# Router weights, gate tiles and gate products rearranged around the end of a mixer and the ranking of a mixture of experts

## Chip, cores and metric

One core of a Trainium2 chip runs the whole kernel as one program. The metric is the device time of one execution in microseconds (us).

## The reference

Two decoder layers over 256 tokens of 1024 channels, all in float32. A layer is a token mixer (differential attention and latent attention, merged by sigmoid gates), a layer norm, and a channel mixer with a gated embedding input. The channel mixer is a dense SwiGLU in layer 0 and a top-2-of-8 mixture of experts in layer 1:

```python
x = layernorm(ALPHA * x + mixer(x))            # ln_mix
h = swiglu(x) or moe(x)                        # layer 0 / layer 1
e = sigmoid(x @ w_ple_gate) * (p @ w_ple_proj) # gated embedding
x = layernorm(ALPHA * x + h + e)               # ln_ffn
```

The mixture takes logits = x @ w_router, the two largest of each token, and softmax gates; each expert is a SwiGLU of width 3584.

## The kernel before

**Products.** Float32 accuracy comes from splitting each operand into a high part (float32r, a cast on ScalarE) and a low part (the remainder, a subtraction on VectorE), and adding three products (`mm3`, L116): one of 128x512 columns is 12 instructions for four blocks of 128 channels. A weight tile is 128x2048 (1 MB): `fetch` (L88) issues its load on the SP queue into one of four raw buffers, `parts` (L97) makes its high part (three buffers) and low part (two buffers), in halves. `stream` (L109) does both. A raw buffer is free again when its low part has been made, a low buffer when the products that read it are over.

**Order.** Outside `manual_schedule` a planner places each instruction on its engine by estimated costs and due times, so work can be drawn ahead of or into other work. Inside `manual_schedule` the instructions keep the order written, but planned ones can be placed between them. Engines run their own instructions in order.

**End of the mixer** (L619 to L645, both layers). The output projection adds w_out tiles into four PSUM banks `yo`. In a manual block: the second half of these products, `ple_product` (L764, 24 products of the embedding, four PSUM banks `prps`), then on VectorE for the two token blocks (tb) the residuals (L340), the start of the norm (L357), the root (L371, eight small steps) and the scaling (L374), which writes x.

**Layer 0 after it** (L1343 to L1352). `transpose_x` (L302) turns x block by block on TensorE and splits it. `ple_out` (L773) copies the embedding sums out of PSUM, which frees the banks that the gate products need. `ple_gate` (L799) streams the four tiles of w_ple_gate, with 24 products each for the two token blocks, and `gate_add` (L782) applies sigmoid and product and adds to x. Then the dense SwiGLU (L806).

**Layer 1 after it** (`before_moe`, L887, all in a manual block). In this order: the router weights are loaded on POOL's queue and split; x is turned and split; the router's 24 products (L904); high parts of the gate tiles on ScalarE, around `ple_out`; `choose` (L933: logits out of PSUM, turned, the two largest); `counts` (L961: five small products); `rank` (L977: experts sorted by load, written as integers `meta`); the low parts of all four gate tiles; `begin` (L1055), which issues the first six expert loads; the 96 gate products; `places` and `select` (which token goes where); the split of x for the gathers; `gate_add`.

**Experts.** An expert's address is read by SP from `meta`, so no expert load can be issued before `rank`. The six raw buffers (four and two extra) give six loads ahead. `run` (L1105) first gathers the tokens of the first pair, then makes high parts four steps and low parts three steps ahead of the products (`cast_hi` L1089, `cast_lo` L1097), and each step asks for one more load (`more`, L1063). There are eight jobs of 42 tiles, small (8 products a tile) and large (12 products a tile); the first is small. In the last job's end the residual sums are combined and the result is normalised and stored.

Memory of closed pools is given to new ones; an instruction that writes to such a place waits for the readers of the old tile.

Of the kernel before, what the change touches and what calls it, by code (L numbers as in the profile page):

```python
# [10 lines left out]
F32 = mybir.dt.float32  # L11
F32R = mybir.dt.float32r
# [8 lines left out]
D = 1024  # L21
# [56 lines left out]
class Net:  # L78
# [18 lines left out]
    def parts(self, raw, a, b):  # L97
        nc = self.nc
        hi = self.wp.tile([128, 2048], F32R, name="whi", tag="whi", bufs=HI_BUFS)
        lo = self.wp.tile([128, 2048], F32R, name="wlo", tag="wlo", bufs=LO_BUFS)  # L100
        step = max(1, self.width // b) * b
        for c0 in range(0, a * b, step):
            s = slice(c0, min(c0 + step, a * b))
            self.latest = nc.scalar.copy(hi[:, s], raw[:, s])  # L104
            with self.after(self.hold.pop() if self.hold else None):
                nc.vector.tensor_tensor(lo[:, s], raw[:, s], hi[:, s], op=OP.subtract)  # L106
        return [[t[:, k * b:(k + 1) * b] for k in range(a)] for t in (hi, lo)]
# [35 lines left out]
    def start(self):  # L143
# [12 lines left out]
        vec = self.vec = cp.tile([12, 128], F32, name="vec")  # L156
        for r0, nr, nm in ((0, 6, "mla_q_norm_g"), (6, 4, "mla_kv_norm_g"), (10, 2, "diff_subln_g")):
            nc.sync.dma_start(vec[r0:r0 + nr], i[nm].rearrange("l (a p) -> (l a) p", p=128))
# [243 lines left out]
    def mixer(self, l):  # L402
# [182 lines left out]
        self.ple_load(l)  # L585
        mh = mp.tile([128, KC, T], F32R, name="mh", tag="dq")
# [24 lines left out]
        def wout(k0, g):  # L611
            return self.stream(self.rows(i["w_out"][l], k0, 4, g * 512, 512), 4, 512)
# [12 lines left out]
        w = [wout(4, g) for g in range(2)]  # L625
# [3 lines left out]
        with self.tc.manual_schedule():  # L629
# [3 lines left out]
            self.ple_product()  # L633
# [9 lines left out]
            self.ln_root(1)  # L643
            for c in range(2):
                self.ln_scale(1, b, u, c)  # L645

# [117 lines left out]
    def ple_product(self):  # L764
        w, p = self.ple
        self.prs = {}
        for tb in range(2):
            for g in range(2):
                ps = self.prs[tb, g] = self.mmp.tile([128, 512], F32, name="prps", tag="mm")
                gs = slice(g * 512, (g + 1) * 512)  # L770
                self.xs(ps, [w[0][:, k, gs] for k in range(2)], [w[1][:, k, gs] for k in range(2)], 0, 2, tb, 2, p)

    def ple_out(self):  # L773
        pr = self.mp.tile([128, 2, D], F32, name="pr")
        for (tb, g), ps in self.prs.items():
            self.nc.scalar.copy(pr[:, tb, g * 512:(g + 1) * 512], ps)
        return pr
# [21 lines left out]
    def ple_gate(self, l, pr):  # L799
        for g in range(2):  # L800
            pss = self.gate_ps()
            for n in (2 * g, 2 * g + 1):
                self.gate_mm(pss, self.stream(*self.gate_tile(l, n)), n)
            self.gate_add(pr, pss, g)
# [69 lines left out]
    def route_tables(self):  # L874
# [10 lines left out]
        self.fold = rp.tile([128, 64], F32, name="fold")  # L885

    def before_moe(self, l, xp):  # L887
        nc, mp, rp, j = self.nc, self.mp, self.rp, l // 2
        self.hold, self.first = [], []
        rw = mp.tile([128, KC, NE], F32, name="rw")  # L890
        nc.gpsimd.dma_start(rw, self.rows(self.i["router_w"][j], 0, KC, 0, NE))
        self.route_tables()
        raws = [self.fetch(*self.gate_tile(l, n)) for n in range(4)]
        self.xp, self.turn = xp, 0
        rwh, rwl = (mp.tile([128, KC, NE], F32R, name=nm) for nm in ("rwh", "rwl"))
        self.split(rwh, rwl, rw)
        nc.vector.tensor_tensor(self.fold, self.ident[:, 0:64], self.ident[:, 64:128], op=OP.add)
# [5 lines left out]
        for k in range(KC):  # L903
            self.mm3(rps[:NE, :T], rwh[:, k], rwl[:, k], self.xh[:, k, :], self.xl[:, k, :], k == 0, k == KC - 1)  # L904
        his, los = ([self.side(nm, F32R, n, own, extra) for n in range(4)]
                    for nm, own, extra in (("whi", HI_BUFS, XHI_BUFS), ("wlo", LO_BUFS, XLO_BUFS)))
        for n in range(2):
            nc.scalar.copy(his[n], raws[n])
        pr = self.ple_out()
        for n in range(2, 4):  # L910
            nc.scalar.copy(his[n], raws[n])
        m, gg, eq = self.choose(rps)
        nc.scalar.activation(gg[:, :, 1:2], gg[:, :, 1:2], AF.Exp)
        cps = self.counts()
        self.rank(cps)
        for n in range(4):
            nc.vector.tensor_tensor(los[n], raws[n], his[n], op=OP.subtract)
        self.begin(j)
        gws = [[[t[n][:, k * 512:(k + 1) * 512] for k in range(4)] for t in (his, los)] for n in range(4)]
        pss = [self.gate_ps() for _ in range(2)]  # L920
        for n in range(4):
            self.gate_mm(pss[n // 2], gws[n], n)
        self.places(cps, m, gg, eq)
        self.sel = rp.tile([128, 2, NP, 256], F32R, name="sel", tag="sel")
        self.select(0)
        self.xth = rp.tile([128, 2, D], F32R, name="xth")
# [3 lines left out]
        for g in range(2):  # L930
            self.gate_add(pr, pss[g], g)
# [123 lines left out]
    def begin(self, j, jobs=None, ahead=RAW_BUFS + XRAW_BUFS):  # L1055
# [3 lines left out]
        self.raws, self.expert = [], {}  # L1059
# [45 lines left out]
    def run(self, done=None, pairs=True):  # L1105
# [6 lines left out]
        self.his, self.los = [], []  # L1112
# [53 lines left out]
        for s in range(ah):  # L1166
            self.cast_hi(s)
            if s < al:
                self.cast_lo(s)
# [157 lines left out]
def body(tc, ins, consts, out, tap=None):  # L1327
# [5 lines left out]
    with pool("const") as cp, pool("small") as sp, pool("weights") as wp, \  # L1333
            tc.tile_pool(name="mm", bufs=MM_BUFS, space=PSUM) as mmp, tc.tile_pool(name="at", bufs=8 - MM_BUFS, space=PSUM) as ap:
        n.cp, n.sp, n.wp, n.mmp, n.ap = cp, sp, wp, mmp, ap
        with pool("bias") as n.bp, pool("xt") as n.tp:
            for l in range(DEPTH):
# [4 lines left out]
                if l % 2 == 0:  # L1342
                    with pool("ffn") as n.mp:  # L1343
                        n.new_xt()
                        for tb in range(2):
                            n.transpose_x(tb)
                        pr = n.ple_out()
                        n.tap(f"x{2 * l}", n.x)
                        n.ple_gate(l, pr)
# [42 lines left out]
```

## Time and profile before

| | us |
|---|---|
| median of 3 runs | 1723.58 (1722.13 to 1727.06) |
| the profiled execution's own time | 1723.58 |
| its span, first to last instruction | 1721.9 |
| TensorE busy | 1639.3 (95%) |
| VectorE busy | 1383.3 (80%) |
| ScalarE busy | 1137.9 (66%) |
| DMA, mean rate over the span | 279 GB/s |

In the profile PE is TensorE's products, PEld its weight loads, DVE VectorE, ACT ScalarE, POOL GpSimd, SP the engine that issues loads. A row names a line of the kernel, an operation, and out<-in by the program's names; what stands in brackets is how long the engine had been idle and what released it. PEclk is the granted share of TensorE's full clock. All times are from the start of the span.

### The profile page before, as it was taken

The page shows a single profiled execution, that of the slowest core. Times are in us where ns is not written, and L with a number is a line of the kernel's source. Part 1 is how long each engine was busy: PE and PEld are TensorE (multiplying, and loading weights), DVE is VectorE, ACT ScalarE, POOL GpSimd, SP SyncE. Part 2 cuts the span into 40 slices and gives each one's busy share as a digit, 9 for nine tenths or more (in the row PEclk, how much of TensorE's full clock was granted, in tenths as well). Part 3 has the DMA queues.
Part 4 walks back from the last instruction along what each step waited for, and adds up shares of the span by engine and source line. Part 5 has one row for each costly group of instructions (what it writes and reads, how often), then busy time and mean ns, then how long its engine had stood idle before and what let it go on. Part 6 is the DMA issues. An engine that isn't in the chain of part 4 may idle for free.

```text
span 1721.9 us, 22472 instructions
## 1 busy us (share of the span) xinstructions
PE 1639.3 (95%) x8152; PEld 1343.8 (78%) x8152; DVE 1383.3 (80%) x1687; ACT 1137.9 (66%) x1366; POOL 43.0 (2%) x39
## 2 busy tenths in 40 slices
PE   8899998999989999978999999999999999999995
PEld 8787787888878887856778887788888877788874
DVE  6987776544567678677999889998888898998997
ACT  5556744434446667347888778877777788777884
POOL 0321000000000000000000000000000000000000
PEclk9999999999989999989999999999999999999998
DMA  7434464555546444635999999999999999999993
GB/s 253 156 123 138 150 214 154 195 185 189 176 131 206 131 151 138 235 147 224 409 403 405 348 380 402 403 409 351 353 367 354 377 399 392 409 406 360 405 404 148
DMA packets 171584, 481.25 MB, mean 279 GB/s; under 512 B 8876, under 2 KB 33592, under 8 KB 171464
## 3 DMA queue, kind: packets, MB, share of 16 engines
q1 hardware_dynamic: 170120, 474.98, 74.3%
q0 software_dynamic: 1344, 4.75, 0.9%
q8 instruction: 66, 1.08, 0.3%
q14 instruction: 54, 0.44, 0.1%
HBM read 478.65 MB, written 1.05 MB: 279 GB/s over the span
## 4 chain that ended last, share of the span: by engine, by line
PE 34%; DMA 9%; DVE 6%; ACT 3%; issue 1%; DVEq 0%; ACTq 0%; SPq 0%
DMA raw<-in_expert_w_dram 9%; PE mps L118 6%; PE mps L120 6%; PE mps L119 5%; DVE wlo L1102 5%; PE macc L118 3%; PE macc L120 3%; PE macc L119 3%; ACT whi L1094 2%; PE mps L1040 2%; PE mps L1041 2%; PE ftp L1240 1%; PE macc L1040 1%; PE macc L1041 1%; PE htp L1244 1%
## 5 line engine op out<-in xcount | busy, mean ns | idle before, releaser
L1102 DVE TENSOR_TENSOR wlo<-raw,whi 128x2048 fp32r<-128x2048 f32 (+1 forms) x338 | 756.4, 2272 | 48.7 <-ACT whi L1094 29.6
L1094 ACT CAST whi<-raw 128x2048 fp32r<-128x2048 f32 (+1 forms) x338 | 637.9, 1907 | 146.6 <-DMA raw<-in_expert_w_dram 58.5
L106 DVE TENSOR_TENSOR wlo<-raw,whi 128x1024 fp32r<-128x1024 f32 (+2 forms) x222 | 259.5, 1190 | 158.0 <-issue 79.3
L104 ACT CAST whi<-raw 128x1024 fp32r<-128x1024 f32 (+2 forms) x222 | 218.6, 1015 | 183.1 <-PE hps L120 51.8
L1040 PE MATMUL mps<-wlo,g 128*128 128x512 f32 x448 | 181.3, 405 | 9.4 <-DVE wlo L1102 7.6
L118 PE MATMUL mps<-wlo,g 128*128 128x512 f32 x448 | 178.2, 398 | 0.4 <-DVE wlo L1102 0.4
L120 PE MATMUL mps<-whi,g 128*128 128x512 f32 x448 | 176.6, 394 | 0.0
L1041 PE MATMUL mps<-whi,g 128*128 128x512 f32 x448 | 176.5, 394 | 0.0
L119 PE MATMUL mps<-whi,g 128*128 128x512 f32 x448 | 175.7, 392 | 0.0
L1040 PEld LDWEIGHTS mps<-wlo,g 128*128 128x128 f32 x448 | 84.6, 189 | 39.2 <-DVE wlo L1102 21.8
L1040 PE MATMUL macc<-wlo,hi 128*128 128x512 f32 x224 | 92.9, 415 | 13.6 <-DVE hi L127 10.9
L120 PEld LDWEIGHTS mps<-whi,g 128*128 128x128 f32 x448 | 84.1, 188 | 20.0
L118 PEld LDWEIGHTS mps<-wlo,g 128*128 128x128 f32 x448 | 84.2, 188 | 19.1 <-DVE wlo L1102 1.1
L119 PEld LDWEIGHTS mps<-whi,g 128*128 128x128 f32 x448 | 84.2, 188 | 18.8
L1041 PEld LDWEIGHTS mps<-whi,g 128*128 128x128 f32 x448 | 84.8, 189 | 17.3
L400 PE MATMUL dqp<-x,whi 128*128 128x512 f32 x256 | 95.6, 414 | 2.2 <-DVE vm L484 2.2
L1041 PE MATMUL macc<-whi,hi 128*128 128x512 f32 x224 | 89.7, 401 | 0.0
L118 PE MATMUL macc<-wlo,hi 128*128 128x512 f32 x224 | 88.6, 395 | 0.0
L120 PE MATMUL macc<-whi,lo 128*128 128x512 f32 x224 | 88.1, 393 | 0.0
L119 PE MATMUL macc<-whi,hi 128*128 128x512 f32 x224 | 87.8, 392 | 0.0
L118 PE MATMUL hps<-wlo,x 128*128 128x512 f32 (+1 forms) x192 | 71.8, 374 | 0.0
L120 PE MATMUL hps<-whi,x 128*128 128x512 f32 (+1 forms) x192 | 71.4, 372 | 0.0
(371 smaller groups left out, 2945.3 us busy)
## 6 DMA issues: line engine op xcount, KB each, us to landing
raw<-in_expert_w_dram SPq DMA_DIRECT2D x336, 1024.0 KB, 8.7
raw<-in_w_in_dram SPq DMA_DIRECT2D x40, 1024.0 KB, 5.1
raw<-in_dense_w_dram SPq DMA_DIRECT2D x33, 1024.0 KB, 5.1
raw<-in_w_branch_diff_dram SPq DMA_DIRECT2D x8, 1024.0 KB, 5.0
raw<-in_w_out_dram SPq DMA_DIRECT2D x8, 1024.0 KB, 5.0
raw<-in_w_ple_gate_dram SPq DMA_DIRECT2D x8, 1024.0 KB, 5.2
raw<-in_w_branch_mla_dram SPq DMA_DIRECT2D x4, 1024.0 KB, 5.3
raw<-in_w_in_dram SPq DMA_DIRECT2D x4, 768.0 KB, 4.8
```

Of the source, the lines that this page charges most:

```text
L104: self.latest = nc.scalar.copy(hi[:, s], raw[:, s])
L106: nc.vector.tensor_tensor(lo[:, s], raw[:, s], hi[:, s], op=OP.subtract)
L118: mm(ps, sh, ml, start=first, stop=False)
L119: mm(ps, sh, mh, start=False, stop=False)
L120: mm(ps, sl, mh, start=False, stop=last)
L400: mm(*one, start=k == 0 and m == 0, stop=end and m == 1)
L1040: mm(ps, st, ml, start=first, stop=False)
L1041: mm(ps, st, mh, start=False, stop=last)
L1094: self.nc.scalar.copy(hi[:, p], raw[:, p])
L1102: self.nc.vector.tensor_tensor(lo[:, p], raw[:, p], self.his[s][:, p], op=OP.subtract)
L1240: nc.tensor.matmul(ps[:, a, q, :], hs[a][n][:, q * 128:(q + 1) * 128], self.fold, start=True, stop=True)
L1244: nc.tensor.transpose(ps[:, q, :], hs[n][:, q * 128:(q + 1) * 128], self.ident)
```

## The change

In layer 0, gate tile 0 is split before the norm and gate tile 1 behind it, at written places; the second of the last two w_out tiles has a low buffer of its own (in memory that the mixer no longer uses); the embedding products are done one token block at a time, with the transposes of x's first block between them; and the gate products of column half 0 run block by block from a manual block. In layer 1, the router weights are loaded in the mixer into a tile of the constants' pool; two gate tiles' high parts and one low part come before the transposes of x; the gate products of tile 0 stand between the router and the ranking, those of the other tiles behind it, with the low parts of tiles 2 and 3 between the steps of the ranking's second half; and the first two expert tiles are split before the experts' loop.

```diff
--- before.py
+++ after.py
@@ -94,10 +94,10 @@
...
-    def parts(self, raw, a, b):
+    def parts(self, raw, a, b, lo=None):
         nc = self.nc
         hi = self.wp.tile([128, 2048], F32R, name="whi", tag="whi", bufs=HI_BUFS)
-        lo = self.wp.tile([128, 2048], F32R, name="wlo", tag="wlo", bufs=LO_BUFS)
+        lo = self.wp.tile([128, 2048], F32R, name="wlo", tag="wlo", bufs=LO_BUFS) if lo is None else lo
         step = max(1, self.width // b) * b
...
@@ -154,6 +154,7 @@
...
         vec = self.vec = cp.tile([12, 128], F32, name="vec")
+        self.rw = cp.tile([128, KC, NE], F32, name="rw")
         for r0, nr, nm in ((0, 6, "mla_q_norm_g"), (6, 4, "mla_kv_norm_g"), (10, 2, "diff_subln_g")):
...
@@ -583,6 +584,8 @@
...
         self.ple_load(l)
+        if not first:
+            nc.gpsimd.dma_start(self.rw, self.rows(i["router_w"][l // 2], 0, KC, 0, NE))
         mh = mp.tile([128, KC, T], F32R, name="mh", tag="dq")
...
@@ -622,7 +625,11 @@
...
                 merged(1)
-        w = [wout(4, g) for g in range(2)]
+        w = [wout(4, 0)]
+        raw = self.fetch(self.rows(i["w_out"][l], 4, 4, 512, 512), 4, 512)
+        w.append(self.parts(raw, 4, 512, mp.tile([128, 2048], F32R, name="wl", tag="kt")))
+        if first:
+            self.gate0 = self.stream(*self.gate_tile(l, 0))
         gbu = mp.tile([128, 2, 2, D], F32, name="gbu", tag="gt")
...
@@ -630,7 +637,10 @@
...
                     self.xs(acc[tb][c], *w[c], 4, 4, tb, KC, (mh, ml))
-            self.ple_product()
+            if first:
+                raw = self.fetch(*self.gate_tile(l, 1))
+            self.prs = {}
+            self.ple_product(0)
             for c in range(2):
...
@@ -641,8 +651,14 @@
...
             self.ln_root(1)
+            if first:
+                self.new_xt()
+                self.transpose_x(0)
+            self.ple_product(1)
             for c in range(2):
                 self.ln_scale(1, b, u, c)
+            if first:
+                self.gate1 = self.parts(raw, 4, 512)
...
@@ -761,20 +777,16 @@
...
-    def ple_product(self):
+    def ple_product(self, tb):
         w, p = self.ple
-        self.prs = {}
-        for tb in range(2):
-            for g in range(2):
-                ps = self.prs[tb, g] = self.mmp.tile([128, 512], F32, name="prps", tag="mm")
-                gs = slice(g * 512, (g + 1) * 512)
-                self.xs(ps, [w[0][:, k, gs] for k in range(2)], [w[1][:, k, gs] for k in range(2)], 0, 2, tb, 2, p)
-
-    def ple_out(self):
-        pr = self.mp.tile([128, 2, D], F32, name="pr")
-        for (tb, g), ps in self.prs.items():
-            self.nc.scalar.copy(pr[:, tb, g * 512:(g + 1) * 512], ps)
-        return pr
+        for g in range(2):
+            ps = self.prs[tb, g] = self.mmp.tile([128, 512], F32, name="prps", tag="mm")
+            gs = slice(g * 512, (g + 1) * 512)
+            self.xs(ps, [w[0][:, k, gs] for k in range(2)], [w[1][:, k, gs] for k in range(2)], 0, 2, tb, 2, p)
+
+    def ple_out(self, pr, tb):
+        for g in range(2):
+            self.nc.scalar.copy(pr[:, tb, g * 512:(g + 1) * 512], self.prs[tb, g])
...
@@ -796,12 +808,23 @@
...
-    def ple_gate(self, l, pr):
-        for g in range(2):
+    def ple_gate(self, l):
+        pr = self.mp.tile([128, 2, D], F32, name="pr")
+        with self.tc.manual_schedule():
+            self.ple_out(pr, 0)
             pss = self.gate_ps()
-            for n in (2 * g, 2 * g + 1):
-                self.gate_mm(pss, self.stream(*self.gate_tile(l, n)), n)
-            self.gate_add(pr, pss, g)
+            self.gate_mm(pss, self.gate0, 0, (0,))
+            self.transpose_x(1)
+            self.gate_mm(pss, self.gate1, 1, (0,))
+            self.ple_out(pr, 1)
+            self.gate_mm(pss, self.gate0, 0, (1,))
+            self.gate_mm(pss, self.gate1, 1, (1,))
+        self.tap(f"x{2 * l}", self.x)
+        self.gate_add(pr, pss, 0)
+        pss = self.gate_ps()
+        for n in (2, 3):
+            self.gate_mm(pss, self.stream(*self.gate_tile(l, n)), n)
+        self.gate_add(pr, pss, 1)
...
@@ -883,18 +906,29 @@
...
         self.fold = rp.tile([128, 64], F32, name="fold")
+        nc.gpsimd.tensor_tensor(self.fold, self.ident[:, 0:64], self.ident[:, 64:128], op=OP.add)
...
         self.hold, self.first = [], []
-        rw = mp.tile([128, KC, NE], F32, name="rw")
-        nc.gpsimd.dma_start(rw, self.rows(self.i["router_w"][j], 0, KC, 0, NE))
         self.route_tables()
...
         self.xp, self.turn = xp, 0
+        his, los = ([self.side(nm, F32R, n, own, extra) for n in range(4)]
+                    for nm, own, extra in (("whi", HI_BUFS, XHI_BUFS), ("wlo", LO_BUFS, XLO_BUFS)))
+        gws = [[[t[n][:, k * 512:(k + 1) * 512] for k in range(4)] for t in (his, los)] for n in range(4)]
+
+        def high(n):
+            nc.scalar.copy(his[n], raws[n])
+
+        def low(n):
+            nc.vector.tensor_tensor(los[n], raws[n], his[n], op=OP.subtract)
+
         rwh, rwl = (mp.tile([128, KC, NE], F32R, name=nm) for nm in ("rwh", "rwl"))
-        self.split(rwh, rwl, rw)
-        nc.vector.tensor_tensor(self.fold, self.ident[:, 0:64], self.ident[:, 64:128], op=OP.add)
+        self.split(rwh, rwl, self.rw)
+        high(0)
+        low(0)
+        high(1)
         self.new_xt()
...
@@ -902,33 +936,38 @@
...
             self.mm3(rps[:NE, :T], rwh[:, k], rwl[:, k], self.xh[:, k, :], self.xl[:, k, :], k == 0, k == KC - 1)
-        his, los = ([self.side(nm, F32R, n, own, extra) for n in range(4)]
-                    for nm, own, extra in (("whi", HI_BUFS, XHI_BUFS), ("wlo", LO_BUFS, XLO_BUFS)))
-        for n in range(2):
-            nc.scalar.copy(his[n], raws[n])
-        pr = self.ple_out()
-        for n in range(2, 4):
-            nc.scalar.copy(his[n], raws[n])
+        low(1)
+        pr = mp.tile([128, 2, D], F32, name="pr")
+        self.ple_out(pr, 0)
+        pss = [self.gate_ps()]
+        self.gate_mm(pss[0], gws[0], 0, (0,))
         m, gg, eq = self.choose(rps)
+        self.gate_mm(pss[0], gws[0], 0, (1,))
+        self.ple_out(pr, 1)
         nc.scalar.activation(gg[:, :, 1:2], gg[:, :, 1:2], AF.Exp)
...
         self.rank(cps)
-        for n in range(4):
-            nc.vector.tensor_tensor(los[n], raws[n], his[n], op=OP.subtract)
+        high(2)
+        high(3)
         self.begin(j)
-        gws = [[[t[n][:, k * 512:(k + 1) * 512] for k in range(4)] for t in (his, los)] for n in range(4)]
-        pss = [self.gate_ps() for _ in range(2)]
-        for n in range(4):
-            self.gate_mm(pss[n // 2], gws[n], n)
+        self.gate_mm(pss[0], gws[1], 1)
+        low(2)
+        pss.append(self.gate_ps())
+        self.gate_mm(pss[1], gws[2], 2)
         self.places(cps, m, gg, eq)
...
         self.select(0)
+        low(3)
         self.xth = rp.tile([128, 2, D], F32R, name="xth")
...
             self.split(self.xth[:, tb], self.xtl[:, tb], self.x[:, tb])
-        for g in range(2):
-            self.gate_add(pr, pss[g], g)
+        self.gate_mm(pss[1], gws[3], 3)
+        self.gate_add(pr, pss[0], 0)
+        for s in range(2):
+            self.cast_hi(s)
+            self.cast_lo(s)
+        self.gate_add(pr, pss[1], 1)
...
@@ -1056,7 +1095,7 @@
...
         self.blocks, self.steps = self.plan(self.jobs)
-        self.raws, self.expert = [], {}
+        self.raws, self.expert, self.his, self.los = [], {}, [], []
         for _ in range(ahead):
...
@@ -1109,7 +1148,6 @@
...
             last[kind, bi, mat] = s
-        self.his, self.los = [], []
         gs, ups, hid, accs, turn = {}, {}, {}, {}, {}
@@ -1163,7 +1201,7 @@
...
         ah, al = HI_BUFS + XHI_BUFS - 1, LO_BUFS + XLO_BUFS - 1
-        for s in range(ah):
+        for s in range(len(self.his), ah):
             self.cast_hi(s)
...
@@ -1341,12 +1379,7 @@
...
                     with pool("ffn") as n.mp:
-                        n.new_xt()
-                        for tb in range(2):
-                            n.transpose_x(tb)
-                        pr = n.ple_out()
-                        n.tap(f"x{2 * l}", n.x)
-                        n.ple_gate(l, pr)
+                        n.ple_gate(l)
                         n.dense(l // 2)
...
                         n.tap(f"x{2 * l + 1}", n.x)
```

## Rows read from the trace of the kernel before

**Rows 1.** The page, busy time of each engine over the whole span
```profile
PE 1639.3 (95%) x8152; PEld 1343.8 (78%) x8152; DVE 1383.3 (80%) x1687; ACT 1137.9 (66%) x1366; POOL 43.0 (2%) x39
```
**Rows 2.** Stretches, layer 0: length, busy us (xcount) by engine, PEclk, DMA share, GB/s
```profile
272.20:280.00 7.80, 3.36 (x19) 2.39 (x17) 6.23 (x15) 3.33 (x7) 1.05 (x2) 0.76 0.82 230
...
280.00:284.00 4.00, 4.00 (x11) 3.21 (x12) 0.83 (x2) 1.86 (x4) 0.00 (x0) 0.61 0.02 6
```
**Rows 3.** Timeline of TensorE, layer 0: start us, us, instruction, [idle before, releaser]
```profile
277.68 1.97 PE L307 MATMUL xps<-ident,x 128*128 128x128 f32 x8 [2.96 <-DVE x L377]
```
**Rows 4.** Timeline of VectorE, layer 0's norm
```profile
261.61 0.69 DVE L344 SCALAR_TENSOR_TENSOR x<-x,yo 128x512 f32<-128x512 f32 x1 [2.02 <-PE yo L120]
...
263.93 1.22 DVE L106 TENSOR_TENSOR wlo<-raw,whi 128x1024 fp32r<-128x1024 f32 x1
```
**Rows 5.** Timeline of VectorE, layer 1's norm
```profile
726.14 0.69 DVE L344 SCALAR_TENSOR_TENSOR x<-x,yo 128x512 f32<-128x512 f32 x1 [0.81 <-PE yo L120]
...
728.86 0.69 DVE L344 SCALAR_TENSOR_TENSOR x<-x,yo 128x512 f32<-128x512 f32 x1 [2.02 <-PE yo L120]
...
736.75 0.75 DVE L377 SCALAR_TENSOR_TENSOR x<-gbu,ly 128x512 f32<-128x512 f32 x1
...
739.13 1.41 DVE L377 SCALAR_TENSOR_TENSOR x<-gbu,ly 128x512 f32<-128x512 f32 x2
```
**Rows 6.** Timeline of TensorE, layer 1, from the mixer to the experts
```profile
739.54 1.91 PE L307 MATMUL xps<-ident,x 128*128 128x128 f32 x16
...
747.44 0.38 PE L118 MATMUL rps<-x,rwh 128*8 128x256 f32 x1 [5.99 <-DVE x L127]
...
752.40 0.29 PE L939 MATMUL rtp<-ident,lt 8*128 8x8 f32 x2 [0.51 <-DVE lt L936]
...
754.37 0.17 PE L964 MATMUL rkp<-memb,ut 128*128 128x8 bf16 x1 [1.68 <-DVE gg L958]
...
758.89 0.76 PE L118 MATMUL plps<-wlo,x 128*128 128x512 f32 x1 [4.24 <-DVE wlo L917]
...
792.18 0.79 PE L1040 MATMUL mps<-wlo,g 128*128 128x512 f32 x1 [4.81 <-DVE wlo L1102]
```
**Rows 7.** Timeline of POOL and ScalarE, layer 1
```profile
739.82 0.90 POOL L891 DMA_DIRECT2D rw<-in_router_w_dram  x1 [20.28 <-PE prps L120]
...
744.74 0.24 ACT L126 CAST rwh<-rw 128x64 fp32r<-128x64 f32 x1 [7.95 <-DMA rw<-in_router_w_dram]
...
744.89 2.04 ACT L126 CAST x<-xps 128x512 fp32r<-128x512 f32 x4
...
746.80 3.73 ACT L908 CAST whi<-raw 128x2048 fp32r<-128x2048 f32 x2
```
**Rows 8.** Busy time in stretches, layer 1 (columns as in rows 2)
```profile
739.50:741.50 2.00, 1.95 (x17) 1.67 (x15) 1.04 (x2) 0.00 (x0) 1.60 (x5) 1.00 0.03 2
...
774.00:778.00 4.00, 4.00 (x19) 3.21 (x18) 0.69 (x1) 0.00 (x0) 0.00 (x0) 1.00 0.18 70
...
800.00:820.00 20.00, 19.41 (x86) 13.89 (x84) 20.00 (x10) 16.88 (x13) 0.00 (x0) 1.00 1.02 409
```
**Rows 9.** Chain that ended last: start us, us, what
```profile
884.70 0.50 PE macc L1040
```
**Rows 10.** Timeline of ScalarE, layer 0
```profile
267.09 2.01 ACT L104 CAST whi<-raw 128x1024 fp32r<-128x1024 f32 x2 [0.72 <-ACT whi L104]
...
292.66 0.60 ACT L787 ACTIVATE plsg<-plps 128x512 f32<-128x512 f32 x1 [2.12 <-PE plps L120]
```
**Rows 11.** Timeline of VectorE, layer 1, before the experts
```profile
745.50 2.48 DVE L127 TENSOR_TENSOR x<-xps,x 128x512 fp32r<-128x512 f32 x4
...
756.37 0.17 DVE L996 CAST meta<-info 128x16 int32<-128x16 f32 x1
...
756.45 8.89 DVE L917 TENSOR_TENSOR wlo<-raw,whi 128x2048 fp32r<-128x2048 f32 x4
...
769.02 2.35 DVE L127 TENSOR_TENSOR xtl<-x,xth 128x1024 fp32r<-128x1024 f32 x2
```

## The prediction, made before the change was run

> **What bounds the kernel now.** I read the page first, then the two stretches that the change touches, engine by engine. TensorE is busy nearly throughout [rows 1], so a gain can only come from the few places where it stands still or runs slowly, and from the stage at the end that it doesn't bound. There are three.
>
> The first is the end of layer 0's mixer. Between 272.2 and 280.0 TensorE works 3.36 of 7.80 us, its clock falls, and the first 4 us of gate products run at 0.61 of full clock [rows 2]. It waits for the normalised x [rows 3]. VectorE is late because four half tiles of gate weights (the low parts of tiles 0 and 1, 1.22 each, the first of the four in the rows [rows 4]) were planned into the chain of the norm. That makes 4.9 us. The same norm in layer 1 has none of them [rows 5].
>
> The second is in front of the router in layer 1. TensorE has nothing for 5.99 us, since the split of x sits on ScalarE behind the split of the router weights, and these were requested at 739.82 and were there at 744.74 [rows 6, 7]. After the ranking it waits 4.24 us for a gate tile's low part.
>
> The third is the start of the experts. All six raw buffers have been filled by about 775 (70 GB/s from 774 to 778), then the queue stands still until the first expert tile's low part is made at 792.15, which frees the first of them; from there loads run at 409 GB/s with the DMA engines full [rows 6, 8]. A tile of 1.0486 MB takes 2.56 us at that rate, against 8 products of the small job, 8 x 0.227 = 1.8 us (12 products of 512 columns take 728.86 - 726.14 = 2.72 us [rows 5]). So the first job's 42 tiles are paced by the loads. Only from 884.7 is the chain TensorE's without a break [rows 9]; a large job's tile is 12 products, 2.72 us, more than its load. Whatever moves the stream of loads earlier moves the rest with it.
>
> **The change, layer 0.** I carry the undisturbed norm of layer 1 over by the residual of the first token block's second half: 728.86 there, 261.61 here, 467.25 us apart [rows 4, 5]. Nothing in front of that residual moves: tile 1 of the second w_out pair gets a low buffer of its own, and gate tile 0 is split in the buffers so freed, before the norm. VectorE then scales the first block's second half until 270.2 and ends the second root at 271.9. TensorE ends the mixer at 261.6 + 2 x 2.72 = 267.0, does the first block's embedding products (12, until 269.7), four transposes (0.12 each at full clock [rows 6]) until 270.2, the other four until 270.8, and the second block's products until 273.5. ScalarE takes the two high parts of x (0.5 each) until 271.4, gate tile 1's high part (2.0 [rows 10]) until 273.4, and the first copy of the embedding sums (0.5), which frees a PSUM bank at 273.9. VectorE, behind the root, makes two low parts (0.62 each) until 273.1, scales the second block (1.41) until 274.5, and makes tile 1's low part (2.4) until 276.9. So gate products start at 274.0: 12 until 276.7, eight transposes until 277.7, 12 with tile 1 until 280.4, 24 more until 285.9. Before, the sigmoid on those 48 products' end starts at 292.66 [rows 10], so they ended at 292.6. That is 6.7 us; TensorE's pauses shrink to some 0.5 us each. Next in line is gate tile 2's low part, whose buffer comes free at 283.1, 2.4 us of split against 2.7 us of products: covered. I take 6.5. The dense stage and layer 1 keep TensorE busy with a load share well under one, so it carries on.
>
> A rule to weigh here: the change puts transposes between products, and the 16 transposes of layer 1, right behind products, ran at 1.00 of full clock, 1.91 us in all [rows 6, 8]; behind a pause of 2.96 us, eight took 1.97 [rows 3]. The Trainium skill (TensorE: Matmul & The Clock Gate, Part 4: PE-mode transpose) says that transposes don't count as work for the clock. By that the 16 would cost 2 us more here and the products behind them start slowly; the trace speaks against it for a run as short as this.
>
> **Layer 1, up to the ranking** (on the old clock). The router weights' load goes onto POOL's queue behind the embedding load and ahead of the two norm vectors; POOL is idle there for 100 us, so it costs nothing and takes away 739.82 to 744.74. But ScalarE's split of them still can't start before the embedding products end, near 739.5: their tile lies where the old one did, and that one's load waited for those products [rows 7]. From 739.5 ScalarE: 0.24, then two gate high parts ahead of the split of x (1.87 each) until 743.5, then x's four high parts (0.51 each) until 745.5. VectorE: tile 0's low part (2.22 [rows 11]) until 743.9, x's low parts (0.62 each), the third at 745.9. The router starts there instead of 747.44, 1.5 us earlier, and ends 4.45 later (747.44 to 751.89 [rows 6]) at 750.4.
>
> Now the products in between: 12 until 753.1, the ranking's two transposes, 12 more until 755.9 (VectorE's choice, 754.37 - 752.40 = 2.0, hides beside them), then the counts, and 2.2 us of ranking (754.37 to the integers at 756.37 + 0.17 = 756.54 [rows 6, 11]) until 758.2. It was 756.5, so the first expert load is asked for **1.7 us later**. All waiting behind: TensorE has no pause of note, so the clock stays up, where before 24 gate products of tile 0 ran behind a sparse stretch.
>
> **From the ranking to the experts.** TensorE: tile 1 until 761.4, tile 2 until 766.8, tile 3 until 772.3. VectorE: tile 2's low part until 760.4, places and selection (from 756.45 + 8.89 = 765.34 to 769.02 = 3.7 [rows 11]) until 764.1, tile 3's low part until 766.3, x's low parts 2.35 until 768.7, the first gate addition (four steps of 0.69) until 771.5, **expert tile 0's low part until 773.8, tile 1's until 776.1**, the second addition until 778.9, tile 2's until 781.2, then one each 2.3. ScalarE has the high parts earlier in each case. Four of the first loads are issued at 759, the fifth at 760.4 and the sixth at 766.3, when the gate tiles' raw buffers come free, so all six are there at about 776.
>
> Before, load seven went out at 792.15, and 36 loads at 2.56 ended at 884.3. After, loads seven and eight go out at 773.8 and 776.1, load nine at 781.2, and from there 34 at 2.56 end at 868.3. **16.0 us earlier.** The fold matrix moved to POOL, the lists moved to begin, and splitting the calls cost nothing: POOL is idle, and the rest issues nothing new.
>
> Sum: 6.5 + 16.0 = 22.5. The profiled execution took 1723.58 us (span 1721.9), which is the median of the three runs: 1723.6 - 22.5 = **1701**.
>
> **Bounds.** Layer 0: at most 7.6 (20.4 us from 272.2 to 292.6, less 1.9 of transposes and 10.9 of products); at least 3, if ScalarE and clock cost as in the first rival. Loads: at most 17.9 (load seven alone: 792.15 - 773.8 = 18.3, less little), at least 10, if each of VectorE's steps behind the ranking waits once more (two extra low parts, 4.5) and the second addition's 2.8 us leave the queue emptier. Below nothing I exclude for the loads: their start has 16 us in hand.
>
> **Rivals.**
> - *The gate split is still in the way.* Only tiles 0 and 1 are put at fixed places; tile 2's high part is planned freely, and in the trace it already sits at 267.09 in the norm [rows 10]. Ahead of the copies that free PSUM it costs 2.0 us, TensorE pauses 2.6 us and starts slowly (at 0.61 over 4 us, 1.6 us). Layer 0 gives 3: about 1704.5. Chance 0.13.
> - *Transposes hold the clock down*, the page's rule as a mechanism: 2 us for 16 at the slow row's 0.246 each and 1.6 for the products behind: 1704.7. For it, the slow row; against it, the row at 1.00. Chance 0.05.
> - *The stream is paced from its first load, not from the freed buffer.* Then the ranking's 1.7 us count against it: 1723.6 - 6.5 + 1.7 = 1718.8. Against it, the still queue at 774 to 778. Chance 0.06.
> - *Slower: the ranking is held behind the gate products.* Its two transposes and counts queue on TensorE behind 24 products. At half clock these take 5.4 us more, and if tile 0's low part or a PSUM bank is late, the loads wait for all of it. The ranking comes 7 us late that way; it decides once it comes more than 16 us late, after about 774.5, since until then the freed buffer is the later one, and it must eat layer 0's gain as well: near 1730. For it, the clock of 0.61 behind a pause; against it, the 16 us in hand. Chance 0.03.
>
> **Chances.** The forecast 0.73; the four above 0.13, 0.05, 0.06, 0.03. A measurement of this kernel tells 0.3%, 5.2 us, from no change. The forecast and the first two lie far beyond it; the third (4.8 us) lies at the line and goes mostly to "same". Faster 0.93, same 0.04, slower 0.03. The range reaches up over the first two rivals and a poor case of the loads (6.5 + 10 less some of layer 0: 1711), down to 7.6 + 17.9: 1697 to 1711.
>
> **What would show it.** In layer 0: no low parts of gate weights between the residuals and the last scaling, gate products from about 274 at full clock, the 48th over near 286. In layer 1: the router about 1.5 us earlier by the mixer's end, the ranking's integers slightly later, the first expert low part about 18 us earlier, load seven likewise, no still stretch of the queue over 3 us, and the chain passing to TensorE for good some 16 us (with layer 0, 22) earlier. Wrong would be: a pause in front of the gate products in layer 0, the experts' first low part no earlier, or a stream whose end doesn't move with its restart.

## The result, and the profile after

The changed kernel takes 1706.62 us (median of 4, 1706.16 to 1707.80) against 1722.86 (4 runs) before: a ratio of 0.9902, 95% interval 0.9885 to 0.9919, 16.2 us less. The forecast was 22.5 less, and its range holds the result. The profiled execution's span fell from 1721.9 to 1705.0, by 16.9.

To see where these 16.9 us come from I cut each execution at three events: VectorE's first step on the queries in layer 0's mixer (29.98 before), the second residual in layer 1 (728.86, [rows 5]), and the end of the first expert job's wait for loads (TensorE at 884.70, [rows 9]).

| us | first step to residual (layer 0) | residual to first job's end | from there to the end |
|---|---|---|---|
| before | 698.9 | 155.8 | 837.2 |
| after | 695.6 | 141.7 | 837.0 |
| change | -3.3 | -14.1 | -0.2 |
| forecast | -6.5 | -16.0 | 0 |

The first column holds all of layer 0 and layer 1's mixer. Against the sum of the changes, 17.6, the span fell by 0.7 less, since the first step came 0.7 us later, in a place that no edit touches. Both gains came, both short.

**Layer 0, after.** TensorE, ScalarE and VectorE in time order (columns as in rows 3), then two stretches (as in rows 2):

```profile
276.61 0.50 PE L118 MATMUL plps<-wlo,x 128*128 128x512 f32 x1 [2.20 <-ACT pr L789]
281.05 1.04 PE L308 MATMUL xps<-ident,x 128*128 128x128 f32 x8
```
```profile
271.00 1.29 ACT L126 CAST x<-xps 128x512 fp32r<-128x512 f32 x2 [0.75 <-PE xps L308]
272.19 3.89 ACT L104 CAST whi<-raw 128x1024 fp32r<-128x1024 f32 x4
275.98 1.07 ACT L789 COPY pr<-prps 128x512 f32<-128x512 f32 x2
...
290.32 0.60 ACT L799 ACTIVATE plsg<-plps 128x512 f32<-128x512 f32 x1 [0.67 <-PE plps L120]
```
```profile
274.00:276.60 2.60, 0.42 (x2) 0.00 (x0) 2.60 (x4) 2.60 (x5) 1.05 (x2) 1.00 0.28 107
276.60:281.00 4.40, 4.39 (x12) 3.45 (x13) 0.74 (x1) 0.45 (x1) 0.00 (x0) 0.61 0.94 277
```

The four half low parts are out of the norm, and VectorE was on time. The pause of 2.96 us [rows 3] became one of 2.20 us, released now by ScalarE's first copy. In front of that copy stand *four* half high parts, 3.89 us: those of gate tile 1, as written, and two more, of gate tile 2, that the planner put there. The first 12 products then took 4.44 us (276.61 to 281.05) for the 2.72 of a full clock, which was granted at 0.61, a mean of its two levels: behind the pause most products came 0.43 us apart (half clock, 1.2 GHz), the last ones 0.23. The 48th product was over at 290.3, against 292.6, although this execution's first step came 0.7 us later.

**Layer 1, after.** TensorE, ScalarE and VectorE up to the experts, and TensorE where the first job ends:

```profile
743.02 0.38 PE L118 MATMUL rps<-x,rwh 128*8 128x256 f32 x1 [4.14 <-DVE x L127]
...
750.96 0.29 PE L978 MATMUL rtp<-ident,lt 8*128 8x8 f32 x2
...
867.98 0.80 PE L1079 MATMUL macc<-wlo,hi 128*128 128x512 f32 x1 [2.44 <-DVE hi L127]
```
```profile
736.71 0.24 ACT L126 CAST rwh<-rw 128x64 fp32r<-128x64 f32 x1 [2.49 <-PE prps L118]
736.87 3.70 ACT L922 CAST whi<-raw 128x2048 fp32r<-128x2048 f32 x2
...
771.11 0.60 ACT L799 ACTIVATE plsg<-plps 128x512 f32<-128x512 f32 x1 [2.20 <-PE plps L120]
```
```profile
726.29 0.69 DVE L345 SCALAR_TENSOR_TENSOR x<-x,yo 128x512 f32<-128x512 f32 x1 [2.02 <-PE yo L120]
...
756.03 0.17 DVE L1035 CAST meta<-info 128x16 int32<-128x16 f32 x1
756.12 2.29 DVE L925 TENSOR_TENSOR wlo<-raw,whi 128x2048 fp32r<-128x2048 f32 x1
...
769.22 4.49 DVE L1141 TENSOR_TENSOR wlo<-raw,whi 128x2048 fp32r<-128x2048 f32 x2
...
777.10 13.30 DVE L1141 TENSOR_TENSOR wlo<-raw,whi 128x2048 fp32r<-128x2048 f32 x6 [0.74 <-ACT whi L1133]
```

Counted from the residual: the router starts 1.9 us earlier (16.7 against 747.44 - 728.86 = 18.6), released by VectorE and no longer by the load [rows 7]; the ranking's integers come 2.2 us later (29.7 against 27.5); the first expert low part is over 18.1 us earlier (769.22 + 2.29 - 726.29 = 45.2 against 63.3). The seventh load went out at 771.53, the eighth at 773.73, the ninth only at 779.42, behind the second gate addition. The stretches (last columns: PEclk, DMA share, GB/s) show what that cost:

```profile
777.00:779.00 2.00, 1.30 (x6) 0.75 (x4) 1.90 (x1) 2.00 (x3) 0.00 (x0) 1.00 1.02 410
779.00:781.00 2.00, 1.55 (x7) 1.28 (x8) 2.00 (x2) 2.00 (x2) 0.00 (x0) 1.00 0.70 164
781.00:783.00 2.00, 1.94 (x9) 1.27 (x8) 2.00 (x2) 2.00 (x2) 0.00 (x0) 1.00 0.85 322
...
785.00:787.00 2.00, 1.89 (x9) 1.26 (x8) 2.00 (x2) 2.00 (x4) 0.00 (x0) 1.00 1.09 297
...
791.00:793.00 2.00, 1.92 (x9) 1.24 (x8) 2.00 (x2) 1.72 (x1) 0.00 (x0) 1.00 1.04 422
```

The queue is full at 410 GB/s until 779, a stretch in which it had stood still before [rows 8]; then it sinks to 164 and takes ten us to fill again.

### The profile page after: what moved, and what is told of

Read it like the earlier page. It is cut to its first block, busy times and chain, and to the rows that moved or that the text cites. A ratio compares the mean times of both kernels' runs of the same rounds, so it can differ in the third digit from the quotient of the medians.

```text
span 1705.0 us, 22467 instructions
## 1 busy us (share of the span) xinstructions
PE 1639.5 (96%) x8152; PEld 1345.3 (79%) x8152; DVE 1383.5 (81%) x1686; ACT 1137.8 (67%) x1366; POOL 43.8 (3%) x40
## 4 chain that ended last, share of the span: by engine, by line
PE 42%; DMA 7%; DVE 6%; ACT 3%; issue 1%; DVEq 0%; ACTq 0%; SPq 0%
DMA raw<-in_expert_w_dram 7%; PE mps L118 6%; PE mps L120 6%; PE mps L119 6%; DVE wlo L1141 4%; PE macc L118 3%; PE mps L1079 3%; PE macc L120 3%; PE macc L119 3%; PE mps L1080 3%; ACT whi L1133 2%; PE ftp L1278 2%; PE macc L1079 1%; PE macc L1080 1%; PE htp L1282 1%
## 5 line engine op out<-in xcount | busy, mean ns | idle before, releaser
L106 DVE TENSOR_TENSOR wlo<-raw,whi 128x1024 fp32r<-128x1024 f32 (+2 forms) x218 | 254.6, 1190 | 149.0 <-issue 78.9
L1079 PEld LDWEIGHTS mps<-wlo,g 128*128 128x128 f32 x448 | 84.7, 189 | 35.1 <-DVE wlo L1141 17.6
L118 PEld LDWEIGHTS mps<-wlo,g 128*128 128x128 f32 x448 | 84.2, 188 | 18.3 <-DVE wlo L1141 0.2
L118 PE MATMUL macc<-wlo,hi 128*128 128x512 f32 x224 | 88.6, 395 | 0.0
```

Source lines behind the costliest of these rows:

```text
L118: mm(ps, sh, ml, start=first, stop=False)
L1079: mm(ps, st, ml, start=first, stop=False)
```

## The experiments

In layer 0, theory 1 says that gate tile 2's high part on ScalarE causes the pause and the slow clock; its rival, theory 2, is that transposes between the products hold the clock down. For the experts, theory 1 says that loads are paced by freed raw buffers, and that VectorE works unbroken from the ranking to the low parts that free them; its rival, theory 2, is the forecast's own statement that a late ranking has 16 us in hand. Each run is compared at the events of the table above.

| us | first step to residual | residual to first job's end | from there to the end | median time |
|---|---|---|---|---|
| after | 695.6 | 141.7 | 837.0 | 1706.6 |
| 1, layer 0 alone | 695.7 | 156.5 | 836.9 | 1719.9 |
| 2, layer 1 alone | 698.8 | 141.9 | 837.0 | 1709.9 |
| 3, tile 2 fixed | 691.7 | 140.8 | 842.2 | 1704.9 |
| 4, no early split | 695.0 | 146.0 | 836.3 | 1709.5 |
| 5, ranking later | 695.7 | 148.0 | 837.7 | 1713.7 |
| 6, three early | 695.8 | 140.5 | 835.8 | 1706.5 |
| 9, change again | 695.5 | 141.0 | 839.0 | 1707.2 |
| 7, ranking earlier | 695.8 | 142.2 | 837.4 | 1706.1 |
| 8, all three | 692.3 | 139.3 | 836.2 | 1700.6 |
| 10, router weights late | 694.4 | 145.5 | 837.3 | 1708.8 |

**The marks.** The change itself once more, without an edit:

> The changed kernel itself once more, unaltered, on the chip of the three runs beside it: 1706.6 us within 1. It is the mark for runs 7, 8 and 10, and shows how much the load-bound jobs late in the experts differ from one execution to the next.

1707.16 us, single executions from 1699.05 to 1707.73; the last column above differs by up to 6.4 us (835.8 to 842.2) between kernels that are alike there. Part of that arises in late jobs whose loads stand again on the chain that ended last; where the rest arises was not followed. So a difference of a few us is read in the first two columns, not in the time.

**1 and 2, the halves.** Run 1 has the old lines of `before_moe` and of the router weights (first diff), run 2 the old end of the mixer and the old `ple_gate` (second):

```diff
-        self.split(rwh, rwl, self.rw)
-        high(0)
-        low(0)
-        high(1)
+        self.split(rwh, rwl, rw)
+        nc.vector.tensor_tensor(self.fold, self.ident[:, 0:64], self.ident[:, 64:128], op=OP.add)
...
-        self.gate_add(pr, pss[0], 0)
-        for s in range(2):
-            self.cast_hi(s)
-            self.cast_lo(s)
-        self.gate_add(pr, pss[1], 1)
+        for g in range(2):
+            self.gate_add(pr, pss[g], g)
```

```diff
-        w = [wout(4, 0)]
...
-        if first:
-            self.gate0 = self.stream(*self.gate_tile(l, 0))
+        w = [wout(4, g) for g in range(2)]
...
             self.ple_product(0)
+            self.ple_product(1)
...
-            if first:
-                self.gate1 = self.parts(raw, 4, 512)
...
-            self.gate_mm(pss, self.gate0, 0, (0,))
...
+            for n in (2 * g, 2 * g + 1):
+                self.gate_mm(pss, self.stream(*self.gate_tile(l, n)), n)
+            self.gate_add(pr, pss, g)
```

> Only layer 0's part of the change; the router, the ranking and the start of the experts as before. If the two parts add up, this has layer 0's gain as the trace after shows it, 3 us from the second residual to the 48th gate product: 1720 us, with the experts' first low part still near 790. If layer 0's part is worth the 6.5 us predicted and the rest fell short: 1716. If layer 1's part lives on an earlier state of layer 0, the sum of this and the next run misses the whole by more than 3 us.

> Only layer 1's part (router weights ahead, gate products around the ranking, two expert tiles split early); layer 0 as before. Adding up: 1706.6 + 3 = 1709.6 us. If the parts depend on each other, off this by more than 3.

1719.86 (ratio 0.9981, 0.9971 to 0.9990) and 1709.88 (0.9928, 0.9910 to 0.9947). 2.9 and 12.9 us less than the kernel before beside them, 15.8 together: the halves add up, and each shows its gain in its own column alone.

**3, gate tile 2 at a written place.**

```diff
             self.ple_out(pr, 1)
+            raw = self.fetch(*self.gate_tile(l, 2))
             self.gate_mm(pss, self.gate0, 0, (1,))
+            gate2 = self.parts(raw, 4, 512)
             self.gate_mm(pss, self.gate1, 1, (1,))
...
-        for n in (2, 3):
-            self.gate_mm(pss, self.stream(*self.gate_tile(l, n)), n)
+        self.gate_mm(pss, gate2, 2)
+        self.gate_mm(pss, self.stream(*self.gate_tile(l, 3)), 3)
```

> The change, and layer 0's gate tile 2 fetched and split at a written place too, behind the copies that free PSUM. Theory 1 (its high part, drawn in front of these copies on ScalarE, makes TensorE pause 2.2 us and run 12 products at 0.61 of its clock): the copies start 2.0 us earlier, the pause is under 0.7 us, the clock stays at 1.00, and the time falls by 3.5 us, to 1703. Theory 2 (transposes between the products hold the clock down): 12 products still take 4.4 us, and the time falls by at most 2, to 1704.6 or more.

TensorE and ScalarE of this run, and the stretch of the first gate products:

```profile
273.85 0.50 PE L118 MATMUL plps<-wlo,x 128*128 128x512 f32 x1 [0.31 <-ACT pr L789]
276.71 1.03 PE L308 MATMUL xps<-ident,x 128*128 128x128 f32 x8
```
```profile
271.31 2.01 ACT L104 CAST whi<-raw 128x1024 fp32r<-128x1024 f32 x2
273.20 1.08 ACT L789 COPY pr<-prps 128x512 f32<-128x512 f32 x2
```
```profile
274.00:276.60 2.60, 2.60 (x12) 2.14 (x13) 2.46 (x3) 0.28 (x1) 0.68 (x2) 1.00 0.63 222
```

Two half high parts in place of four, a pause of 0.31 us, 12 products in 2.86, the clock at 1.00 all through. Transposes stand between the same products, so runs of eight of them don't hold the clock down here: theory 2 falls. Layer 0's stretch is 3.9 us shorter than after, 7.2 shorter than before. The time fell by only 1.8 (1704.86; 0.9893, 0.9877 to 0.9910, which overlaps with the change): this profile lost 5.2 us behind the first job, where the edit changes nothing. Run 8, with the same edit, has 836.2 there, so the loss doesn't belong to it.

**4, no early split of expert tiles.**

```diff
-        for s in range(2):
-            self.cast_hi(s)
-            self.cast_lo(s)
```

> The change without the two expert tiles split ahead of the experts' loop. Theory 1 (the stream of loads goes on when a raw buffer is freed): the seventh load goes out near 779.3 instead of 771.5, the queue stands still for about 4 us, and the time rises by 4, to 1710.5. Theory 2 (the stream is paced from the first load asked for after the ranking): 1706.6, no change.

1709.49 (0.9922, 0.9905 to 0.9939). The first expert low parts come in one row, as before the change:

```profile
775.51 15.50 DVE L1138 TENSOR_TENSOR wlo<-raw,whi 128x2048 fp32r<-128x2048 f32 x7 [3.93 <-ACT whi L1130]
```

The seventh load goes out at 777.83, the first job ends 4.3 us later than after: freed buffers pace the stream, and theory 2 falls. But counted from the residual the seventh load is 7.7 us later (53.0 against 45.2), and only the tenth is later by as much as the job's end (59.6 against 55.3); the paragraph on all runs below comes back to it. The two splits are worth 4.3 of the 14.1 us. The other 9.8 are what is left for the router, the gate products and the placing of the steps; of these, run 10 prices the early load of the router weights.

**5, a later ranking.**

```diff
         self.gate_mm(pss[0], gws[0], 0, (1,))
+        self.gate_mm(pss[0], gws[1], 1)
         self.ple_out(pr, 1)
...
         self.begin(j)
-        self.gate_mm(pss[0], gws[1], 1)
         low(2)
```

> The change, with gate tile 1's 24 products ahead of the counts too, so that the ranking comes 5.5 us later. The prediction's reading (the loads have 16 us in hand before a late ranking counts): 1706.6, no change. Theory 1 (VectorE works without a pause from the ranking to the low parts that free the raw buffers, so a late ranking is passed on in full): the first expert tile's low part 5.5 us later, TensorE pauses about 4 us for gate tile 2's low part, and the time rises by 5 to 7, to 1712 to 1714.

1713.72 (0.9954, 0.9938 to 0.9969): 7.1 us more. VectorE's rows:

```profile
774.83 4.49 DVE L1141 TENSOR_TENSOR wlo<-raw,whi 128x2048 fp32r<-128x2048 f32 x2
...
783.64 6.69 DVE L1141 TENSOR_TENSOR wlo<-raw,whi 128x2048 fp32r<-128x2048 f32 x3 [1.67 <-ACT whi L1133]
```

The ranking's integers and the first low part are 5.6 us later than after; the third low part is 6.5 later, and the first job ends 6.3 later. Nothing was in hand. TensorE paused 4.15 us for gate tile 2's low part, which VectorE makes behind the ranking, so the gate products, and ScalarE's work behind them, came late as well; this run alone doesn't tell which of the two delays counted.

**6, three expert tiles early.**

```diff
-        for s in range(2):
+        for s in range(3):
             self.cast_hi(s)
```

> The change with three expert tiles split early instead of two, the second gate addition behind them. Theory 1 (after the change the stream still loses some 2.5 us between 779 and 789, where the ninth load waits for the second gate addition and too few loads are under way): the ninth load goes out near 776 instead of 779.4, no 2 us stretch below 390 GB/s, and the time falls by 2.5, to 1704. Theory 2 (a queue that is filled one load per low part is slow whatever the ninth does): within 0.5 us of the change.

1706.51. The ninth load goes out at 776.19, 3.2 us earlier, but the tenth at 781.05 instead of 781.62, behind the gate addition that now stands after three low parts. The first job ends 0.5 to 1.2 us sooner (140.5 against 141.0 and 141.7), about as much as the tenth load is earlier counted from the residual (0.8). The queue still ran below 390 GB/s, at 315, 385, 365 and 305 in the four stretches from 781 to 789. So theory 1 has the right wait, but its time, 1704, and its full queue did not come; the time is theory 2's. The gap moved one load on.

**7, an earlier ranking.**

```diff
-        self.gate_mm(pss[0], gws[0], 0, (0,))
         m, gg, eq = self.choose(rps)
-        self.gate_mm(pss[0], gws[0], 0, (1,))
+        self.gate_mm(pss[0], gws[0], 0, (0,))
         self.ple_out(pr, 1)
...
         cps = self.counts()
+        self.gate_mm(pss[0], gws[0], 0, (1,))
         self.rank(cps)
```

> The change, with the first 12 gate products moved behind the ranking's two transposes and the other 12 of tile 0 behind the counts. Theory 1 (VectorE's unbroken work from the ranking on passes each us of the ranking to the loads): the ranking's integers 2.2 us earlier, load seven 2.2 us earlier, time 2 us less than the change beside it. The prediction's reading (16 us in hand): no difference.

1706.12, against 1707.16 for the change beside it, and the first job's end no sooner (142.2 against 141.0 and 141.7). The ranking's integers were 2.2 us earlier and load seven went out at 769.57; theory 1's expectation was wrong all the same. VectorE, then ScalarE:

```profile
777.85 4.49 DVE L1141 TENSOR_TENSOR wlo<-raw,whi 128x2048 fp32r<-128x2048 f32 x2 [3.45 <-ACT whi L1133]
```
```profile
771.87 0.60 ACT L799 ACTIVATE plsg<-plps 128x512 f32<-128x512 f32 x1 [2.20 <-PE plps L120]
...
775.84 10.95 ACT L1133 CAST whi<-raw 128x2048 fp32r<-128x2048 f32 x6
```

The third expert tile's low part waits 3.45 us for its high part, which ScalarE makes behind the copies of the gather, and these wait for TensorE's last gate products, no sooner than in the change (771.9 against 771.1). In the change that wait is 0.74 us: two chains, VectorE's from the ranking and TensorE's gate products with ScalarE's copies behind, end there almost together. A later ranking cost about all of its delay (run 5), an earlier one gained nothing alone.

**8, runs 3, 6 and 7 in one kernel.**

> The change with gate tile 2 at a written place (as run 3), three expert tiles split early (as run 6) and the ranking earlier (as run 7). If the three add up: 3.6 + 1 + 2.2, about 7 us less than the change beside it, 1700. If the load-bound jobs at the end take back what comes early: the first job's end 7 us earlier in the trace, and the time no more than 3 us less.

1700.61 (0.9871, 0.9856 to 0.9886), 6.6 us less than the change beside it: with three tiles split early their high parts come ahead of the gather's copies, so the earlier ranking now reaches the first job (139.3). Layer 0 gives 3.2 to 3.3, the experts 1.7 to 2.4: 4.9 to 5.7, not the 6.8 of the expected sum. That the time still met the expected 1700 is in part luck: this profile's last column is 2.8 us below that of run 9. It is faster than the kernel before. Against the change, its four executions (1698.89 to 1703.23) lie below the four of the first measurement (1706.16 to 1707.80), but two of the five in run 9 (1699.05, 1701.39) were as fast.

**10, router weights loaded late.** The load stands in `before_moe` again, into a tile of its pool.

```diff
-            nc.gpsimd.dma_start(self.rw, self.rows(i["router_w"][l // 2], 0, KC, 0, NE))
...
+        self.rw = mp.tile([128, KC, NE], F32, name="rw")
+        nc.gpsimd.dma_start(self.rw, self.rows(self.i["router_w"][j], 0, KC, 0, NE))
```

> The change with the router weights loaded where the kernel before loads them, behind the mixer. Theory 1: their load lands near 741.6, two gate tiles' high parts wait behind their split on ScalarE, the router starts 4.9 us later, and all of it is passed on: 1711.5. If the loads had time in hand: 1706.6.

ScalarE, and TensorE's first router product:

```profile
738.99 0.24 ACT L126 CAST rwh<-rw 128x64 fp32r<-128x64 f32 x1 [7.87 <-DMA rw<-in_router_w_dram]
```
```profile
745.29 0.38 PE L118 MATMUL rps<-x,rwh 128*8 128x256 f32 x1 [9.52 <-DVE x L127]
```

The router starts 22.1 us after the residual instead of 16.7, and the first job ends 3.8 to 4.5 later. The time rose by 1.7 only (1708.81; 0.9923, 0.9908 to 0.9938). Against run 9 this profile's first step came 1.8 us sooner, its first column is 1.0 shorter and its last 1.7, so the two profiled executions took the same (1707.86 and 1707.73); no run ties these three to the edit.

**All runs together.** The tenth load, before and after:

```profile
798.76 0.37 SPq L94 DMA_DIRECT2D raw<-in_expert_w_dram  x1
```
```profile
781.62 0.37 SPq L94 DMA_DIRECT2D raw<-in_expert_w_dram  x1
```

| us behind the second residual | seventh load | tenth load | first job's end | from the tenth load to it |
|---|---|---|---|---|
| before | 63.3 | 69.9 | 155.8 | 85.9 |
| after | 45.2 | 55.3 | 141.7 | 86.4 |
| 4, no early split | 53.0 | 59.6 | 146.0 | 86.4 |
| 5, ranking later | 50.7 | 61.7 | 148.0 | 86.3 |
| 6, three early | 45.2 | 54.5 | 140.5 | 86.1 |
| 7, ranking earlier | 43.1 | 55.9 | 142.2 | 86.3 |
| 8, all three | 43.1 | 53.7 | 139.3 | 85.6 |
| 9, change again | 45.2 | 55.3 | 141.0 | 85.6 |
| 10, router weights late | 49.6 | 59.7 | 145.5 | 85.8 |

The first job's end stands 85.6 to 86.4 us behind the tenth load in all nine (in runs 1 to 3 it is 86.8, 86.5 and 85.6); from the seventh it varies from 92.5 to 99.1. The tenth load goes out when the fourth expert tile's low part is made, and from there VectorE makes one each 2.2 us. So what an edit is worth is read at the tenth load, and the seventh, by which the forecast and the expectations of runs 4 and 7 went, says little. No run moves the tenth load alone.

## Why the prediction was right, and where it was off

- **Layer 0: right in mechanism, off in size, by the first rival.** "gate tile 1's high part (2.0 [rows 10]) until 273.4, and the first copy of the embedding sums" failed: tile 2's high part, 2 us more, stood there too. The rival priced it: 2.0 us, a pause of 2.6 (2.20 measured), slow products for 1.6 (4.44 - 2.72 = 1.7 measured), 3 us left: 3.3 came. Run 3 takes away that one thing and gives 7.2, run 8 gives 6.6, where the sum said 6.7. The rival's 1704.5 and the 1.9 us by which the loads fell short make 1706.4; the profiled execution took 1706.71. I gave it a chance of 0.13, though the row at 267.09 [rows 10] showed the planner doing just this, and nothing in the change stopped it.
- **Transposes and the clock.** Wrong as a rival: 8 took 1.03 us between products, and with no pause in front the clock stayed at 1.00 (run 3). The Trainium skill (TensorE: Matmul & The Clock Gate, Part 4: PE-mode transpose) says that transposes don't count as busy time for the clock in the way that products do. For runs of eight between products, and for the 16 behind products in layer 1 (1.91 us at 1.00 [rows 6, 8]), the measured rows show no loss from it.
- **Router.** 1.5 us earlier forecast, 1.9 measured. ScalarE's split did wait for the embedding products (2.49 us, released by them), as read from the load that had to wait [rows 7].
- **Ranking.** 1.7 us later forecast, 2.2 measured.
- **Seventh load.** 18.3 us earlier forecast, 18.1 measured. But it was the wrong load to go by: the tenth came 14.6 us earlier, and the first job's end 14.1.
- **Loads.** "from there 34 at 2.56" failed: the sum took the ninth load's stream as full at once. It went out 0.8 us later than that sum would have it on this clock, and from its issue to the job's end are 88.6 us (867.98 - 779.42), not the 87.0 of 34 loads and the 0.4 that the old kernel needed beyond its 36 (884.70 - 884.3). That is 1.1 more: 0.4 of it lies between the tenth load and the job's end (86.4 against 85.9), and 0.7 is the sum's own, which let the queue fill at as little cost from the ninth load as it had from the seventh. 0.8 and 1.1 make the 1.9 between 16.0 and 14.1.
- **"their start has 16 us in hand" (of the loads).** Wrong, and the sum's own steps contradict it: they run without a gap from the ranking to the first low part. Run 5 showed a first load asked for 5.6 us later as 5.6 us of low part and 6.3 us at the first job's end (7.1 of time). The fourth rival's threshold was therefore wrong too; run 5's late ranking cost some 1.1 us per us. The error did no harm to the sum, which had passed the ranking's delay on.
- **Carried on.** The last stretch stayed within 0.2 us in this pair. But it varies by some us between executions, so a measured time holds less than the trace. And the chain is not TensorE's without a break from 884.7 on, as the prediction had it: in the kernel before, loads stand on it again in later jobs, such as this one (a row of the chain that ended last):

```profile
1471.50 12.80 DMA raw<-in_expert_w_dram
```

- **The range.** Its lower end, 1697, is 1 us below its own terms (1723.6 - 7.6 - 17.9 = 1698.1). It held the result because it reached over the first rival; the forecast itself, 1701, was 5.6 us too low.

## What to carry to other kernels

When work is put at a written place to clear a chain, look at every planned piece that is free to move into the gap, on each engine of the chain: the next tile will. A wait of several engines that end close together yields nothing to the one that is hurried; find the second chain's slack (0.74 us here) before pricing the first. And if a queue is paced by freed buffers, count which load each step frees, and find the load that the end follows: here it was the tenth, and moving the seventh and eighth alone did nothing for it (run 7).

## What was not expected of the hardware

After the change the queue, down to 164 GB/s from 779 to 781, was slow to fill while one load was asked for every 2.2 us: 322, 297 and at last 422 GB/s over some ten us, at a DMA share up to 1.09 with less moved. Before the change the queue, empty since about 776, was back at 369 GB/s in its second two us (794 to 796, share 0.93) and at 401 in its third, but then fell to 363 and 387. Over the ten us behind the load with which it started again the two differ little: 318 GB/s before (from 792.16), 300 after (from 779.42), against 409 when full. Why a queue with a share near 1 moves less in such a stretch stays open.
